# Longer stretches of projection matmuls for the DeltaNet inputs and gates, and the last columns of the final norm's product on GpSimd, in a hybrid attention and DeltaNet block

## The chip, the cores and the metric

The kernel runs on one core of a Trainium2 chip. The metric is the device time of one execution in microseconds. A core has five engines that run at the same time, each with an instruction queue of its own: TensorE (PE in the profile; its weight loads are listed apart as PEld), VectorE (DVE), ScalarE (ACT), GpSimd (POOL) and SyncE (SP), which here issues the transfers between the chip's memory (HBM) and the core's own memories. Those are SBUF, 128 partitions wide, and PSUM, into which TensorE writes.

## The reference

One decoder block for 1,024 tokens of width 1,024. The normed input is projected once. Half of the columns goes through stick-breaking attention with 8 heads, the other half through a gated DeltaNet with 4 heads; both are normed by head, gated, joined and projected back, the input is added, and a last norm follows.

```python
h = rmsnorm(x, norm1_w)
proj = einsum('btd,de->bte', h, w_in)
sb_q, sb_k, sb_v, sb_z, g_q, g_k, g_v, g_z, g_b, g_a = split(proj)

# attention, per query block of 128: A = sigmoid(z) * prod(1 - sigmoid(z) of the keys between)
o_sb = rmsnorm(stick_breaking_attention(sb_q, sb_k, sb_v), sb_norm_w) * silu(sb_z)

# DeltaNet: causal convolution of 4 taps, silu, l2 norm, then chunk by chunk
v_new = u_c - w_c @ state
o_c = (q_c * exp(g_c)) @ state + a_c @ v_new
state = state * exp(g_last) + (k_c * exp(g_last - g_c)).T @ v_new
o_gdn = rmsnorm(o_gdn, gdn_norm_w) * silu(g_z)

x = x + concat(o_sb, o_gdn) @ w_out
return rmsnorm(x, final_norm_w)
```

The kernel takes chunks of 128 tokens in the DeltaNet instead of 64. Everything is in 32-bit floats. The large products run in a reduced form: each operand is split into a high and a low part, and three products replace one.

## The kernel before

**Stages.** The queries (stage Q), half of the values and the decay inputs are projected first. Then a long middle part runs four kinds of work side by side on TensorE: the remaining projections, the DeltaNet's preparation and its recurrence over eight chunks per head, and attention window by window. Last comes the output product, one block of 128 tokens after another, first the DeltaNet's half of the columns, then attention's.

**Projections.** `projections` (line 889) goes through the list `ORDER` (line 29): G0 to G3 are the inputs of the four DeltaNet heads (three blocks of columns each), k0 to k3 the keys, z4 to z7 the gates of the DeltaNet, z0 to z3 the gates of attention, v1 the second half of the values. One block is two halves of 512 tokens; one half is eight steps k of three matmuls each (`mm3`), all into one PSUM buffer `pp` (for G0's second half `pz`). In the order rows they read `pp<-xh,weh`, `pp<-xl,weh` and `pp<-xh,wel`. A half has 24 such matmuls.

**What sets the order.** The program's generators are run by a planner, `interleave` (line 440). It holds a model of the engines with a cost for each operation. Each kind of work is a `Stream` with a priority. A stream runs until its next `yield`; then, when the modelled TensorE has nothing queued, the planner takes the ready stream of best priority. A stream is ready when the results that it waits for have been there in the model for `SLACK` = 450 ns. The projections (`fill`, line 1568) have priority 100, behind the recurrence (0), its preparation and attention (10): they are what TensorE does while the others wait. Where a projection yields is therefore where other work may cut in. Line 942 sets this: after every second step k (six matmuls), for z0 to z3 after every step (three matmuls). The planner's order on TensorE is the order of the program; on the other engines the modelled order is laid down in the same way.

**Names in the middle part.** `gdn_chain` (line 1195) is the recurrence: per chunk `pc<-state,kqf` and `pz<-state,kqf` (products with the state), `pc<-xct,xinv` (the solve), `pz<-v,kn` (the state's update) and `pz<-vr,at` (the output). These are full 32-bit matmuls, which the profile lists as two records each. `window` (line 1291) is attention: `pz<-kh,q` and `pz<-kl,q` are scores, `pz<-step,stf` transposes of the weights (`step` holds the identity), `po<-ah,v2a` and `po<-al,v2a` the products with the values, `pz<-step,otf` the transposes of the output.

**The end.** `products_attention` (line 1517) makes the second half of the output product. For the last block it goes in three pieces of 512, 320 and 192 columns: VectorE adds the piece to the sum in `xr` (`xr<-pp,xr`); ScalarE squares it and sums the squares, for the last piece VectorE (`yj<-xr`, the result in `sy`); and `yf<-xr,fnw` multiplies by the final norm's gain, the first two pieces on GpSimd, the last one on VectorE. GpSimd then takes the root (`ry<-sy,half`), VectorE and ScalarE scale `yf` by it, and two transfers write the block out.

Of the kernel before, what the change touches and what calls it, by code (L numbers as in the profile page):

```python
# [14 lines left out]
ALU = mybir.AluOpType  # L15
# [6 lines left out]
NK = D // P  # L22
# [451 lines left out]
def block(tc, xT_d, x_d, n1_d, wE_d, wQ_d, wC_d, conv_d, alog_d, dtb_d, mixw_d, wo_d, fnw_d, out_d):  # L474
    nc = tc.nc
    ck = Model({"V": nc.vector, "A": nc.scalar, "G": nc.gpsimd, "P": nc.tensor, "S": nc.sync})
    V, A, G, TE, S = ck.V, ck.A, ck.G, ck.P, ck.S

    with ExitStack() as top:
# [36 lines left out]
        def rsqrt(y, a, n):  # L516
            return G.tensor_tensor(y, a, half[:, 0:n], ALU.pow)
# [68 lines left out]
        def mm3(out, lh, ll, rh, rl, start, stop):  # L586
            TE.matmul(out, lh, rh, start=start, stop=False)
            TE.matmul(out, lh, rl, start=False, stop=False)
            TE.matmul(out, ll, rh, start=False, stop=stop)
# [50 lines left out]
        for k in range(NK):  # L640
# [29 lines left out]
            if k:  # L670
                for j in range(8):
                    i, hs = j // 2, slice((j % 2) * 512, (j % 2) * 512 + 512)
# [97 lines left out]
        def values():  # L770
            for b in range(NB):
                yield lambda: ps.room("pp", 2)
                bs = slice(b * P, (b + 1) * P)
                pt = pp()
                for k in range(NK):
                    mm3(pt[:, 0:256], xh[:, k, bs], xl[:, k, bs], chl[k][:, 0, 264:520], chl[k][:, 1, 264:520], k == 0, k == NK - 1)
                    if k % 2 and k < NK - 1:
                        yield
                v_evac(pt, b, 0, 4, 1.0)
                yield  # L780
            flags["v1"] = True
# [107 lines left out]
        def projections():  # L889
            todo = []  # L890
            for step in ORDER:
                if step[0] == "G":
                    h = int(step[1])
                    todo += [(f"G{h}{kind}", lambda: True) for kind in (1, 0, 2)]
                else:
                    todo.append((step, lambda: True))

            def take():
                for n, (name, ok) in enumerate(todo):
                    if ok():  # L900
                        del todo[n]
                        if name[0] == "v":
                            return name, None
                        e = {"k": 0, "z": 16}.get(name[0])
                        e = 4 + 4 * int(name[2]) + int(name[1]) if name[0] == "G" else e + int(name[1])
                        if e == early.e:
                            return name, early
                        cols = Columns(e)
                        cols.load()
                        return name, cols  # L910
                return None

            def split(nxt, n):
                while nxt and nxt[1] and len(nxt[1].hl) < n:
                    nxt[1].split()

            nxt = take()
            split(nxt, 2)
            while nxt:
                name, cols = nxt  # L920
                if name[0] == "v":
                    nxt = take()
                    split(nxt, 2)
                    yield from values()
                    continue
                fill.prio = 100
                for half in range(2):
                    hs = slice(half * 512, (half + 1) * 512)
                    wide = name[:2] == "G0" and half
                    yield lambda: ps.room("pz", 4) if wide else ps.room("pp", 2)  # L930
                    pt = pz() if wide else pp()
                    for k in range(NK):
                        n = 8 * half + k
                        if n == 2:
                            nxt = take()
                        if n == 8:
                            split(nxt, 1)
                        if n == 12:
                            split(nxt, 2)
                        h, l = cols.hl[k // 4]  # L940
                        mm3(pt, h[:, k % 4, :], l[:, k % 4, :], xh[:, k, hs], xl[:, k, hs], k == 0, k == NK - 1)
                        if (k % 2 or name in ('z0', 'z1', 'z2', 'z3')) and k < NK - 1:
                            yield
                    if half == 0:
                        if name[0] == "G":
                            ev = g_evac(int(name[1]), int(name[2]))
                        else:
                            ev = {"k": k_evac, "z": z_evac}[name[0]](int(name[1]))
                    flags[name if half else name + ".0"] = ev(pt, half)
                    yield  # L950
                if nxt is None:
                    nxt = take()
                    if nxt is None and todo:
                        yield lambda: any(ok() for _, ok in todo)
                        nxt = take()
                    split(nxt, 2)
            flags["proj"] = True
# [412 lines left out]
        wts = {}  # L1370
# [56 lines left out]
        def block_tile(b, name):  # L1427
            return pools[0].tile([P, D], F32, tag="xr", bufs=3, name=name) if b < 3 else pools[1].tile([P, D], F32, tag="yr", bufs=5, name=name)
# [88 lines left out]
        def products_attention():  # L1517
            yield lambda: f"d{NB - 1}" in flags
            for b in range(NB):
                last = b == NB - 1  # L1520
                parts = (slice(0, 512), slice(512, 832), slice(832, D)) if last else (slice(0, 512), slice(512, D))
                sy = None
                for got in product(b, 0, parts):
                    if not isinstance(got, tuple):
                        yield got
                        continue
                    n, hs, yp, y = got
                    if sy is None:
                        sy = pools[0].tile([P, 3], F32, tag="sy", bufs=2, name="sy")
                        yf = block_tile(0, "yf") if last else y  # L1530
                    V.tensor_tensor(y[:, hs], yp, y[:, hs], ALU.add)
                    junk = pools[1].tile([P, 584], F32, tag="yj", name="yj")
                    if n == 2:
                        V.scalar_tensor_tensor(junk[:, 0:hs.stop - hs.start], y[:, hs], 1.0 / D, y[:, hs], ALU.mult, ALU.mult, accum_out=sy[:, n:n + 1])
                    else:
                        A.activation(junk[:, 0:hs.stop - hs.start], y[:, hs], AF.Square, scale=D ** -0.5, accum_out=sy[:, n:n + 1])
                    if last and n < 2:
                        G.tensor_tensor(yf[:, hs], y[:, hs], wts["fnw"][:, hs], ALU.mult)
                    if n == 1 and last:
                        G.tensor_tensor(sy[:, 0:1], sy[:, 0:1], sy[:, 1:2], ALU.add)  # L1540
                    elif n:
                        V.scalar_tensor_tensor(sy[:, 0:1], sy[:, 0:1], EPS, sy[:, n:n + 1], ALU.add, ALU.add)
                    if n < len(parts) - 1:
                        yield
                        continue
                    if last:
                        V.tensor_tensor(yf[:, hs], y[:, hs], wts["fnw"][:, hs], ALU.mult)
                    ry = pools[0].tile([P, 1], F32, tag="ry", bufs=2, name="ry")
                    os_ = slice(b * P, (b + 1) * P)
                    if last:  # L1550
                        rsqrt(ry, sy[:, 0:1], 1)
                        V.tensor_scalar(yf[:, 0:640], yf[:, 0:640], ry[:, 0:1], None, ALU.mult)
                        A.activation(yf[:, 640:D], yf[:, 640:D], AF.Copy, scale=ry[:, 0:1])
                        S.dma_start(out_d[os_, 0:640], yf[:, 0:640])
                        nc.scalar.dma_start(out_d[os_, 640:D], yf[:, 640:D])
                    else:
                        rsqrt(ry, sy[:, 0:1], 1)
                        for u in range(2):
                            us = slice(512 * u, 512 * u + 512)
                            yb = (pc, po)[u]()  # L1560
                            A.activation(yb, y[:, us], AF.Copy, scale=ry[:, 0:1])
                            V.tensor_tensor(y[:, us], yb, wts["fnw"][:, us], ALU.mult)
                        S.dma_start(out_d[os_, :], y)
                    ck.free(*ready[b, 0][:2], y)
                    flags[f"a{b}"] = True
                    yield
# [46 lines left out]
```

## Time and profile before

| | |
|---|---|
| median of 3 runs | 648.09 us (647.86 to 648.28) |
| the profiled execution | 648.12 us |
| its span, first to last instruction | 646.0 us |
| granted TensorE clock, mean | 0.999 |
| HBM traffic | 76.03 MB read, 35.03 MB written, 172 GB/s |

The span is what the profile covers; the execution's own time has 2.1 us more around it. In a row of the timeline stand the start in us, the duration in us, the engine, the line, the operation, the tile written and those read, the shape, how many records are merged (x2), and in brackets how long the engine sat idle before and what ended that. Almost all rows carry line 358, where a recorder passes every operation on, so groups are told apart by their tiles. In a row of groups stand the busy time in us and the mean of one in ns, then idle time. In a row of waits stand who waited for whom, us in total, how often, and the longest.

TensorE is busy from the first slice of the span to the last but one. The granted clock is full throughout. The transfers take 53.5% of the 16 DMA engines' time.

### The profile page before, as it was taken

The numbers are of one execution on the slowest core, as the hardware profiler recorded it, in microseconds if no ns is written. First come the engines' busy times: TensorE is split into PE (matmuls) and PEld (weight loads), VectorE is DVE, ScalarE is ACT, GpSimd is POOL, SyncE is SP. The second block draws the span as 40 slices with busy tenths as digits, with TensorE's granted clock in tenths as the row PEclk, the third lists the DMA queues.
The fourth block names the chain that finished last, engine by engine and source line by source line (L and its number), as shares of the span: only waits on it lengthen the run. The fifth ranks groups of instructions, "written<-read, shape, count | busy, mean of one in ns | idle before, by whom it ended". The sixth has DMA issues, their size and how long they took to land.

```text
span 646.0 us, 11666 instructions
## 1 busy us (share of the span) xinstructions
PE 637.4 (99%) x3976; PEld 549.4 (85%) x3976; DVE 425.0 (66%) x779; ACT 394.0 (61%) x945; POOL 339.2 (53%) x428
## 2 busy tenths in 40 slices
PE   8999999999999999999999999999999999999996
PEld 7889988988888898888988888988888887888885
DVE  4469974223897768887658777585774237468864
ACT  5764577724968778787668677585654342132553
POOL 0115056837793668974486955667432232136632
PEclk9999999999999999999999999999999999999999
DMA  8886338766472553654445734636222279773223
GB/s 292 320 282 234 132 118 293 266 206 209 140 228 86 159 182 93 222 157 143 117 150 142 236 116 118 207 101 190 86 62 89 80 247 316 288 227 99 66 102 126
DMA packets 96666, 111.82 MB, mean 173 GB/s; under 512 B 28576, under 2 KB 61536, under 8 KB 96608
## 3 DMA queue, kind: packets, MB, share of 16 engines
q1 hardware_dynamic: 96320, 110.89, 53.5%
q8 instruction: 31, 0.51, 0.3%
q14 instruction: 27, 0.22, 0.1%
q10 hardware_dynamic: 288, 0.20, 0.1%
HBM read 76.03 MB, written 35.03 MB: 172 GB/s over the span
## 4 chain that ended last, share of the span: by engine, by line
PE 92%; DVE 3%; ACT 2%; issue 1%; POOL 1%; DMA 1%; POOLq 0%; SPq 0%; DVEq 0%; ACTq 0%
PE pp L358 54%; PE pz L358 27%; PE po L358 7%; PE pc L358 3%; DVE mgf L358 1%; POOL rsb L358 1%; ACT nkv L358 0%; DMA mgf<-gate_s 0%; DVE ssb L358 0%; DVE xr L358 0%; DVE mf L358 0%; ACT xinv L358 0%; ACT sgf L358 0%; DMA xr<-x 0%; DVE al L358 0%
## 5 line engine op out<-in xcount | busy, mean ns | idle before, releaser
L358 PE MATMUL pp<-xh,weh 128*128 128x512 f32 x360 | 148.1, 411 | 0.0
L358 PE MATMUL pp<-xh,wel 128*128 128x512 f32 x360 | 141.4, 393 | 0.0
L358 PE MATMUL pp<-xl,weh 128*128 128x512 f32 x360 | 140.6, 391 | 0.0
L358 POOL TENSOR_TENSOR sgf<-sgf,cc 128x128 f32<-128x128 f32 (+3 forms) x64 | 77.3, 1210 | 56.9 <-DVE cc L358 52.8
L358 POOL TENSOR_TENSOR wel<-wer,weh 128x512 fp32r<-128x512 f32 x48 | 62.6, 1307 | 74.6 <-ACT weh L358 65.3
L358 PEld LDWEIGHTS pp<-xh,wel 128*128 128x128 f32 x360 | 67.5, 188 | 15.4
L358 PEld LDWEIGHTS pp<-xl,weh 128*128 128x128 f32 x360 | 67.8, 188 | 10.8
L358 PEld LDWEIGHTS pp<-xh,weh 128*128 128x128 f32 x360 | 67.6, 188 | 10.8 <-DVE ac L358 0.2
L358 DVE TENSOR_TENSOR_SCAN cc<-pz,step 128x384 f32<-128x384 f32 (+2 forms) x64 | 53.6, 847 | 13.1 <-ACT pz L358 8.7
L358 DVE TENSOR_TENSOR al<-pz,ah 128x512 fp32r<-128x512 f32 (+1 forms) x80 | 49.6, 631 | 18.9 <-ACT ah L358 18.5
L358 ACT ACTIVATE ah<-pz 128x512 fp32r<-128x512 f32 (+1 forms) x80 | 43.7, 565 | 24.1 <-PE pz L358 23.1
L358 ACT ACTIVATE sgf<-pz,rs 128x384 f32<-128x384 f32 (+3 forms) x96 | 54.5, 601 | 4.9 <-PE pz L358 4.6
L358 ACT ACTIVATE pz<-pz,ns 128x384 f32<-128x384 f32 (+3 forms) x96 | 53.2, 583 | 0.0
L358 PE MATMUL pp<-woh,mh 128*128 128x512 f32 (+2 forms) x132 | 51.8, 393 | 0.6 <-DMA mgf<-gate_s 0.5
L358 PE MATMUL pp<-woh,ml 128*128 128x512 f32 (+2 forms) x132 | 50.9, 386 | 0.0
L358 PE MATMUL pp<-wol,mh 128*128 128x512 f32 (+2 forms) x132 | 50.6, 383 | 0.0
L358 PE MATMUL po<-ah,v2a 128*128 128x256 f32 (+1 forms) x160 | 43.9, 300 | 0.0
L358 POOL TENSOR_TENSOR ml<-mf,mh 128x512 fp32r<-128x512 f32 x16 | 21.5, 1346 | 42.2 <-ACT mh L358 37.7
L358 DVE TENSOR_TENSOR_SCAN cc<-pz,cc,step 128x512 f32<-128x512 f32 (+1 forms) x32 | 38.8, 1213 | 6.8 <-ACT pz L358 5.9
L358 POOL TENSOR_TENSOR ac<-ac,pre 128x512 f32<-128x512 f32 x24 | 31.0, 1290 | 19.1 <-ACT pre L358 12.9
L358 DVE SCALAR_TENSOR_TENSOR pp<-pre,conv,pp 128x512 f32<-128x512 f32 x42 | 31.5, 750 | 13.7 <-ACT pp L358 13.2
L358 PE MATMUL po<-al,v2a 128*128 128x256 f32 (+1 forms) x160 | 38.7, 280 | 0.0
(292 smaller groups left out, 1590.8 us busy)
## 6 DMA issues: line engine op xcount, KB each, us to landing
wer<-wE SPq DMA_DIRECT2D x48, 256.0 KB, 3.5
xr<-x SPq DMA_DIRECT2D x16, 512.0 KB, 7.9
g_s<-ac SPq DMA_DIRECT2D x24, 256.0 KB, 2.4
v_s<-v2e SPq DMA_DIRECT2D x16, 256.0 KB, 2.6
kqf<-g_s SPq DMA_DIRECT2D x16, 256.0 KB, 3.7
v2a<-v_s SPq DMA_DIRECT2D x8, 512.0 KB, 4.8
q<-qk_s SPq DMA_DIRECT2D x8, 512.0 KB, 5.4
kh<-qk_s SPq DMA_DIRECT2D x8, 512.0 KB, 5.0
```

Source lines behind the costliest of these rows:

```text
L358: ins = f(*args, **kw).ins
```

## The change

Two edits. In `projections`, the streams whose name begins with G or z yield after every fourth step k, that is once in a half, after twelve matmuls; the keys k0 to k3 stay at every second step, and z0 to z3 at every step. In `products_attention`, the last block's third piece of `yf<-xr,fnw` (192 columns) goes to GpSimd as the other two do, and VectorE's instruction for it goes away.

```diff
-                        if (k % 2 or name in ('z0', 'z1', 'z2', 'z3')) and k < NK - 1:
+                        if ((k % 4 == 3 if name[0] in 'Gz' else k % 2) or name in ('z0', 'z1', 'z2', 'z3')) and k < NK - 1:
                             yield
...
-                    if last and n < 2:
+                    if last:
                         G.tensor_tensor(yf[:, hs], y[:, hs], wts["fnw"][:, hs], ALU.mult)
...
-                    if last:
-                        V.tensor_tensor(yf[:, hs], y[:, hs], wts["fnw"][:, hs], ALU.mult)
```

The first edit moves instructions on all engines, since the planner's choices follow each other. On TensorE no matmul is added or removed. Three places show it.

In the middle of the recurrence, here for the second head, TensorE's rows before: a recurrence step (the solve, `xct`), six projection matmuls, the next step (`v`, the state's update) and what follows it.

```order
L358 MATMUL pc_4158<-xct_4160,xinv_826 128x128
L358 MATMUL pp_4163<-xh_110,weh_3920 128x512
L358 MATMUL pp_4163<-xl_111,weh_3920 128x512
L358 MATMUL pp_4163<-xh_110,wel_3921 128x512
L358 MATMUL pp_4163<-xh_110,weh_3920 128x512
L358 MATMUL pp_4163<-xl_111,weh_3920 128x512
L358 MATMUL pp_4163<-xh_110,wel_3921 128x512
L358 MATMUL pz_4185<-v2_4172,kn_2102 128x128
L358 MATMUL pz_4189<-state_3986,kqf12_1427 128x128
L358 MATMUL pz_4189<-vr_4093,at_2200 128x128
```

And TensorE's rows of the change in the same head, from the end of one projection stretch of twelve matmuls on.

```order
L358 MATMUL pp_3817<-xh_110,wel_3664 128x512
L358 MATMUL pz_3906<-v2_3853,kn_2125 128x128
L358 MATMUL pz_3910<-vr_3728,at_2232 128x128
L358 MATMUL po_3816<-ah_3785,v2a_3223 128x256
L358 MATMUL po_3816<-al_3786,v2a_3223 128x256
L358 MATMUL po_3816<-ah_3785,v2a_3223 128x256
L358 MATMUL po_3816<-al_3786,v2a_3223 128x256
L358 MATMUL pz_3978<-step_65,stf66_3770 128x128 x3
L358 MATMUL po_3816<-ah_3875,v2a_3223 128x256
L358 MATMUL po_3816<-al_3876,v2a_3223 128x256
```

Between two stretches, more steps of the recurrence and of attention now stand side by side. Over the whole program TensorE has 97 stretches of projection matmuls instead of 125; before, 101 had six matmuls and 12 had twelve, now 15 have six, 49 have twelve, and 22 have three.

At the end of the last head's recurrence, TensorE's rows before: only projections of z0 to z3 lie between the steps.

```order
L358 MATMUL pc_6739<-state_6723,kqf99_4744 128x128
L358 MATMUL pp_6714<-xh_110,weh_6648 128x512
L358 MATMUL pp_6714<-xl_111,weh_6648 128x512
L358 MATMUL pp_6714<-xh_110,wel_6649 128x512
L358 MATMUL pp_6714<-xh_110,weh_6673 128x512
L358 MATMUL pp_6714<-xl_111,weh_6673 128x512
L358 MATMUL pp_6714<-xh_110,wel_6674 128x512
L358 MATMUL pc_6739<-xct_6741,xinv_826 128x128
```

And the same two steps of the last chunk in the change.

```order
L358 MATMUL pc_6686<-state_6674,kqf91_4761 128x128
L358 MATMUL po_6637<-ah_6654,v2a_6444 128x256
L358 MATMUL po_6637<-al_6655,v2a_6444 128x256
L358 MATMUL po_6637<-ah_6654,v2a_6444 128x128
L358 MATMUL po_6637<-al_6655,v2a_6444 128x128
L358 MATMUL pz_6696<-step_65,stf148_6662 128x128 x4
L358 MATMUL pp_6524<-xh_110,weh_6426 128x512
L358 MATMUL pp_6524<-xl_111,weh_6426 128x512
L358 MATMUL pp_6524<-xh_110,wel_6427 128x512
L358 MATMUL pc_6686<-xct_6688,xinv_826 128x128
```

Attention's last windows (`stf`, `ah`, `al`) now share this part with the recurrence; before, they were finished ahead of it.

The third place is GpSimd's end: before, and then in the change.

```order
L358 TENSOR_TENSOR ry_7879<-sy_7858,half_71 128x1
L358 TENSOR_TENSOR yf_7902<-xr_7088,fnw_7295 128x512
L358 TENSOR_TENSOR yf_7902<-xr_7088,fnw_7295 128x320
L358 TENSOR_TENSOR sy_7901<-sy_7901 128x1
L358 TENSOR_TENSOR ry_7943<-sy_7901,half_71 128x1
```

```order
L358 TENSOR_TENSOR ry_7879<-sy_7858,half_71 128x1
L358 TENSOR_TENSOR yf_7902<-xr_7088,fnw_7295 128x512
L358 TENSOR_TENSOR yf_7902<-xr_7088,fnw_7295 128x320
L358 TENSOR_TENSOR sy_7901<-sy_7901 128x1
L358 TENSOR_TENSOR yf_7902<-xr_7088,fnw_7295 128x192
L358 TENSOR_TENSOR ry_7943<-sy_7901,half_71 128x1
```

The product of 192 columns stands ahead of the root in GpSimd's queue. On VectorE it stood between the square-and-sum `yj` and the last sum `sy`, which now follow each other.

## The prediction

> **What bounds the kernel now.** I read the page's first part, then the chain of waits, then what TensorE itself waited for.
>
> ```profile
> span 646.0 us, 11666 instructions
> PE 637.4 (99%) x3976; PEld 549.4 (85%) x3976; DVE 425.0 (66%) x779; ACT 394.0 (61%) x945; POOL 339.2 (53%) x428
> PE 92%; DVE 3%; ACT 2%; issue 1%; POOL 1%; DMA 1%; POOLq 0%; SPq 0%; DVEq 0%; ACTq 0%
> ```
>
> TensorE is busy for 637.4 of 646.0 us and carries 92% of the chain that ended last. Busy matmul time alone is no proof, because records overlap, so the next view is the list of TensorE's waits:
>
> ```profile
> PE po L358 <- DVE step L358: 1.7, 1, 1.7
> PE pp L358 <- DMA mgf<-gate_s: 0.5, 1, 0.5
> PE pz L358 <- DVE al L358: 0.2, 1, 0.2
> ```
>
> Three waits, 2.4 us, and the largest is the start. So the span is the time to the first matmul, then the sum of the distances from one matmul's start to the next, then a tail:
>
> ```profile
> 1.67 3.36 PE L358 MATMUL po<-step 128*128 128x128 f32 x14 [1.67 <-DVE step L358]
> 639.65 0.28 PE L358 MATMUL pp<-woh,ml 128*128 128x192 f32 x1
> ```
>
> From 1.67 to 639.65 are 638.0 us for 3,975 distances; the tail behind it is 646.0 - 639.65 = 6.35 us. The changed kernel has the same 3,976 matmuls in another order. A reordering can gain only if the distances shrink at the seams between kinds of work, and can lose only by a wait that is new. All sums below are against this execution, 648.12 us with 2.1 us around its span; the median of the runs is 648.09, so nothing needs converting.
>
> **The seams, first edit.** The first half of the change lets a projection of the G and z4 to z7 kind run for twelve matmuls instead of six before other work may come in. The order rows say that it does so: projection stretches on TensorE fall from 125 to 97, those of exactly six from 101 to 15, and 49 are now of exactly twelve. What does a stretch cost? This is the last head's recurrence, in which every step comes between two stretches:
>
> ```profile
> 506.60 0.40 PE L358 MATMUL pp<-xh,wel 128*128 128x512 f32 x1
> 506.83 0.38 PE L358 MATMUL pz<-v,kn 128*128 128x128 f32 x2
> 507.05 0.39 PE L358 MATMUL pz<-state,kqf 128*128 128x128 f32 x2
> 507.27 0.39 PE L358 MATMUL pz<-vr,at 128*128 128x128 f32 x2
> 507.42 0.48 PE L358 MATMUL pp<-xh,weh 128*128 128x512 f32 x1
> 507.73 0.39 PE L358 MATMUL pp<-xl,weh 128*128 128x512 f32 x1
> 507.96 0.39 PE L358 MATMUL pp<-xh,wel 128*128 128x512 f32 x1
> 508.20 0.38 PE L358 MATMUL pc<-state,kqf 128*128 128x128 f32 x2
> ```
>
> The first column is the start, and differences of starts are what count. A projection matmul takes 507.96 - 507.73 = 0.23, but the first one behind the recurrence 507.73 - 507.42 = 0.31: a return seems to cost 0.08 to 0.09. But look at the pairs before it. One pair followed by another takes 507.05 - 506.83 = 0.22, and the last pair only 507.42 - 507.27 = 0.15. What the return adds, the pair has saved. A recurrence pair between two projection stretches costs what it costs among its like, and merging such visits saves about nothing. That is the bulk of the stretches that vanish: of returns behind a 128-wide recurrence pair there are 28 before and 11 now.
>
> Transposes do have a price:
>
> ```profile
> 323.05 0.37 PE L358 MATMUL pz<-step,stf 128*128 128x128 f32 x3
> 323.26 0.46 PE L358 MATMUL pp<-xh,weh 128*128 128x512 f32 x1
> 323.56 0.39 PE L358 MATMUL pp<-xl,weh 128*128 128x512 f32 x1
> 323.79 0.39 PE L358 MATMUL pp<-xh,wel 128*128 128x512 f32 x1
> ```
>
> Three transposes take 0.21, 0.07 each, as always, and the first projection behind them 0.30, so leaving a run of transposes costs 0.07. But it costs that whatever follows, and the number of runs of transposes that end in a projection, score, value or recurrence matmul is 112 in both orders (45, 28, 28 and 11 before; 45, 19, 31 and 17 now). So here too the sum is nil.
>
> I summed the seams in two ways. First, each distance was put into a group by the kinds and widths of the matmul before it, itself and the one behind it, and the middle value of each group laid along both orders: 633.9 us before (the real 638.0 has the start's loads and small lateness on top), 632.2 now, so -1.7; 136 of the 3,975 distances had to be borrowed from the nearest group. Second, each seam between two kinds got its measured excess over the kinds' own pace, and the counts were changed: some 14.3 us of seams in all, and -0.4 for the new counts. The difference between the two is the borrowed groups. I take the middle, **-1.1 us**, with -1.7 and +0.3 as ends (the borrowed distances scatter by 0.05 each, 0.6 over 136).
>
> [...]
>
> **The tail, second edit.** The last 192 columns of the norm's product leave VectorE and go to GpSimd, behind the last block's sum. What stands there now:
>
> ```profile
> 637.66 1.30 POOL L358 TENSOR_TENSOR yf<-xr,fnw 128x512 f32<-128x512 f32 x1 [1.10 <-DVE xr L358]
> 638.69 0.48 DVE L358 TENSOR_TENSOR xr<-pp,xr 128x320 f32<-128x320 f32 x1
> 639.25 0.87 POOL L358 TENSOR_TENSOR yf<-xr,fnw 128x320 f32<-128x320 f32 x1 [0.29 <-DVE xr L358]
> 639.97 0.36 DVE L358 TENSOR_TENSOR xr<-pp,xr 128x192 f32<-128x192 f32 x1 [0.80 <-PE pp L358]
> 640.08 0.20 POOL L358 TENSOR_TENSOR sy<-sy 128x1 f32<-128x1 f32 x1
> 640.46 0.36 DVE L358 SCALAR_TENSOR_TENSOR yj<-xr 128x192 f32<-128x192 f32 x1
> 640.74 0.08 DVE L358 DVE_READ_ACCUMULATOR yj<-xr 128x1 f32 x1
> 640.74 0.35 DVE L358 TENSOR_TENSOR yf<-xr,fnw 128x192 f32<-128x192 f32 x1
> 641.01 0.15 DVE L358 SCALAR_TENSOR_TENSOR sy<-sy 128x1 f32<-128x1 f32 x1
> 641.25 0.54 POOL L358 TENSOR_TENSOR ry<-sy,half 128x1 f32<-128x1 f32 x1 [0.97 <-DVE sy L358]
> 641.82 0.61 ACT L358 ACTIVATE yf<-yf,ry 128x384 f32<-128x384 f32 x1 [1.99 <-POOL ry L358]
> ```
>
> Everything from the root (ry at 641.25) on is the same in both kernels; the question is when ry can start. On VectorE the product delays the sum sy from about 640.95 (0.13 behind the accumulator's 640.82, the distance from xr's end at 640.33 to yj) to 641.01: 0.06. Without a clash, that is all that moving it gains. On GpSimd 512 columns take 1.30 and 320 take 0.87, so 192 take 0.87 - 128 x 0.43/192 = 0.58. GpSimd starts 0.08 behind VectorE's add (639.17 to 639.25), so at 640.41, and ends at 640.99. VectorE's square-and-sum yj, both inputs in SBUF, is due at 640.46, in the middle of it. That the two exclude each other the output stage shows:
>
> ```profile
> 601.88 0.16 DVE L358 SCALAR_TENSOR_TENSOR sy<-sy 128x1 f32<-128x1 f32 x1 [0.85 <-ACT yj L358]
> 613.89 1.29 POOL L358 TENSOR_TENSOR ml<-mf,mh 128x512 fp32r<-128x512 f32 x1 [1.39 <-ACT mh L358]
> 614.11 1.09 DVE L358 SCALAR_TENSOR_TENSOR sy<-sy 128x1 f32<-128x1 f32 x1
> ```
>
> The same one-column sum takes 0.16 alone and 1.09 beside a GpSimd product, ending 0.02 behind it (615.20 against 615.18), that is 0.14 less than its own time later. So yj would end at 640.99 + 0.36 - 0.14 = 641.21, the sum start 0.13 later and end at 641.49, and ry start 0.09 behind that, at 641.58 instead of 641.25: **+0.33**. If VectorE comes first, GpSimd holds ry back to about 641.35: +0.10. If they did not exclude each other: -0.06. I take +0.33, since GpSimd's release is the shorter by 0.05; ends -0.06 and +0.33.
>
> [...]
>
> **The sum:** 648.12 - 1.1 + 0.33 = **647.3 us**. That is 0.8 us or 0.12% under the time before, inside the 0.2% (1.3 us) that a measurement of this kernel can tell from no change.
>
> **The rivals.** *The returns cost what they seem to.* The triple's first matmul has the longer records:
>
> ```profile
> L358 PE MATMUL pp<-xh,weh 128*128 128x512 f32 x360 | 148.1, 411 | 0.0
> L358 PE MATMUL pp<-xl,weh 128*128 128x512 f32 x360 | 140.6, 391 | 0.0
> ```
>
> 20 ns x 360 = 7.2 us over 125 returns are 0.06 each, and measured by starts a whole stretch takes 0.10 longer than its matmuls at their pace. For 28 returns fewer that gives -1.6 to -2.8, with the tail 646.9 to 645.7. Against it stands the short last pair. For it: the grouped sum came out at -1.7.
>
> *A new wait on TensorE; this is the side of slower.* Its place is the end of the last head's recurrence. By the order rows and the distances, attention's last score products move from about 468 to 496 us, while the recurrence ends at 509 instead of 513; before, it had those last 40 us nearly for itself:
>
> ```profile
> 160.00:180.00 20.00, 20.00 (x106) 16.61 (x105) 16.05 (x25) 17.82 (x38) 15.65 (x19) 1.00 0.40 114
> 480.00:500.00 20.00, 20.00 (x134) 18.02 (x133) 9.38 (x21) 8.75 (x27) 2.95 (x5) 1.00 0.21 66
> ```
>
> (Columns: stretch, length, then busy time of PE, PEld, DVE, ACT, POOL.) ScalarE at 8.75 of 20 us would go to the 17 or 18 of the densest stretch, and the only cover there is z0 to z3, which give way every three matmuls, 0.7 us. If six of the last steps each wait 0.5 us, as the output stage's one wait did, that is 3 us: 650.3. It decides from about 2.1 us of new waits. Against it: at 17.82 of 20 us ScalarE made TensorE wait nowhere before, and the shortest distances between a recurrence step and the one that needs its VectorE result are alike in both orders (1.2 us).
>
> That the change would not do what it says is ruled out by the order rows.
>
> **How the numbers follow.** Forecast, within 0.2%: 0.44. Returns that cost what they seem to, with a gain of over 1.3 us: 0.35. New waits that make it slower by over 1.3 us: 0.21. The forecast's own range, from the ends -1.7 - 0.06 and +0.3 + 0.33 with half a microsecond of small waits on top, is 646.3 to 649.3. The range asked for reaches to 645.4 (most of the first rival) and to 650.0 (into the second), and leaves out the rest, some 2 in 10.
>
> **What would show it.** Seams: the sum of distances from first to last matmul falls by about 1 us, with the last start near 638.6; a projection behind a recurrence pair still takes 0.31. Tail: yj on VectorE takes 0.7 instead of 0.36 or starts late, and ry starts 1.9 us behind the last matmul's start instead of 1.60. Wrong: TensorE's list of waits holds more than 4 us, above all at 470 to 515 us, or the distances fall by 2 us or more.

## The result and the profile after

| | before | after |
|---|---|---|
| median | 647.89 us (647.19 to 648.36, 13 runs) | 646.54 us (645.89 to 646.97, 13 runs) |
| ratio, 95% interval | 1 | 0.9978 (0.9970 to 0.9987) |
| span of the profiled execution | 646.0 us | 644.7 us |
| first matmul to last, by starts | 638.0 us | 636.4 us |
| last matmul's start to the end of the span | 6.35 us | 6.67 us |

The last row is worked out from spans given to 0.1 us, here and below.
The changed kernel is 1.35 us faster, 0.2%; 647.3 us were forecast. The head of the page of the changed kernel, and TensorE's list of waits (who waited for whom, us in total, times, longest):

```profile
span 644.7 us, 11693 instructions
PE 635.5 (99%) x3976; PEld 551.4 (86%) x3976; DVE 430.3 (67%) x778; ACT 392.8 (61%) x943; POOL 340.5 (53%) x429
```

```profile
PE po L358 <- DVE step L358: 1.7, 1, 1.7
PE pp L358 <- DVE v2e L358: 0.6, 1, 0.6
PE pz L358 <- DVE oe L358: 0.2, 1, 0.2
```

TensorE still sets the time, and its list of waits is as short as before: 2.5 us against 2.4. The rival of new waits did not come to pass. The 0.6 us for `v2e` lies in the second half of the values, at 118.5 us; in a second trace with the same order of matmuls (the new yields alone, below) it is missing, so it is scatter.

The price of a return to a projection is what the prediction read from before. From the changed kernel's timeline of TensorE (start, duration):

```profile
304.58 0.40 PE L358 MATMUL pp<-xh,wel 128*128 128x512 f32 x1
304.81 0.39 PE L358 MATMUL pz<-v,kn 128*128 128x128 f32 x2
304.96 0.47 PE L358 MATMUL pp<-xh,weh 128*128 128x512 f32 x1
305.27 0.40 PE L358 MATMUL pp<-xl,weh 128*128 128x512 f32 x1
```

The pair takes 0.15 instead of its 0.22, the projection behind it 0.31 instead of 0.23: 0.46 together, 0.01 more than each among its like.

The tail in the changed kernel, from the last matmul on:

```profile
638.03 0.28 PE L358 MATMUL pp<-woh,ml 128*128 128x192 f32 x1
638.34 0.36 DVE L358 TENSOR_TENSOR xr<-pp,xr 128x192 f32<-128x192 f32 x1 [0.80 <-PE pp L358]
638.78 0.59 POOL L358 TENSOR_TENSOR yf<-xr,fnw 128x192 f32<-128x192 f32 x1
638.84 0.75 DVE L358 SCALAR_TENSOR_TENSOR yj<-xr 128x192 f32<-128x192 f32 x1
639.69 0.16 DVE L358 SCALAR_TENSOR_TENSOR sy<-sy 128x1 f32<-128x1 f32 x1
639.93 0.54 POOL L358 TENSOR_TENSOR ry<-sy,half 128x1 f32<-128x1 f32 x1 [0.56 <-DVE sy L358]
```

GpSimd's product takes 0.59 (0.58 was estimated). VectorE's square `yj` is stretched from 0.36 to 0.75 and ends 0.22 behind GpSimd, so the root `ry` starts 1.90 us behind the last matmul's start instead of 1.60. So the second edit costs 0.3 us, and the first has brought 1.6 us of distances. What are these 1.6 us?

### The profile page after: what moved, and what is told of

It is laid out like the page before. It is cut to its first block, busy times and chain, and to the rows that moved or that the text cites. A ratio compares the mean times of both kernels' runs of the same rounds, so it can differ in the third digit from the quotient of the medians.

```text
span 644.7 us, 11693 instructions
## 1 busy us (share of the span) xinstructions
PE 635.5 (99%) x3976; PEld 551.4 (86%) x3976; DVE 430.3 (67%) x778; ACT 392.8 (61%) x943; POOL 340.5 (53%) x429
## 4 chain that ended last, share of the span: by engine, by line
PE 90%; DVE 3%; POOL 3%; issue 1%; ACT 1%; DMA 1%; SPq 0%; POOLq 0%; DVEq 0%; ACTq 0%
PE pp L358 52%; PE pz L358 27%; PE po L358 8%; PE pc L358 3%; DMA dt<-cum_s 1%; DVE cc L358 1%; POOL wel L358 1%; POOL rsb L358 1%; SPq L358 0%; POOL tm L358 0%; DVE ssb L358 0%; POOL ac L358 0%; POOL xs L358 0%; DVE mgf L358 0%; ACT sgf L358 0%
## 5 line engine op out<-in xcount | busy, mean ns | idle before, releaser
L358 PE MATMUL pp<-xh,weh 128*128 128x512 f32 x360 | 146.0, 405 | 0.0
```

The lines of the kernel that those rows point to most:

```text
L358: ins = f(*args, **kw).ins
```

## The experiments

### Each edit alone, and the opposite of the first

The new yields with the old tail, and the old yields with the new tail:

```diff
-                        if (k % 2 or name in ('z0', 'z1', 'z2', 'z3')) and k < NK - 1:
+                        if ((k % 4 == 3 if name[0] in 'Gz' else k % 2) or name in ('z0', 'z1', 'z2', 'z3')) and k < NK - 1:
```

> The new yields alone, with the last product of 192 columns left on VectorE. Theory A (the tail costs what the row of after shows, 6.67 us from the last matmul's start to the end of the span instead of 6.35, and the matmuls' distances are those of the change): 0.3 us less than the whole change, so about 646.2 us, a ratio to before near 0.9974; distances 636.4 us from the first to the last matmul's start, tail 6.35 us. Theory B (the tail's 0.32 us is scatter of one execution): the time of the whole change, 646.5 us.

```diff
-                    if last and n < 2:
+                    if last:
...
-                    if last:
-                        V.tensor_tensor(yf[:, hs], y[:, hs], wts["fnw"][:, hs], ALU.mult)
```

> The old yields, only the last product of 192 columns moved to GpSimd. Theory A: TensorE's order is that of before, so the distances stay near 638.0 us (within 0.4 us), and the tail grows from 6.35 to 6.67 us: 0.3 us slower than before, about 648.2 us, ratio 1.0005. Theory B (product on GpSimd beside the square is worth something): not slower than before. [...]

Measured: 646.43 us, ratio 0.9982 (0.9973 to 0.9991), for the yields alone; distances 636.7, tail 6.39. And 648.23 us, ratio 1.0009 (1.0000 to 1.0018), for the tail alone; distances 637.5, tail 6.66. Theory A holds for the tail in both traces. The times are too coarse to tell it from theory B: the yields alone have the ratio 0.9982, the whole change 0.9978. The distances of one order scatter by up to half a microsecond between traces, nearly all of it in the projections of queries and values: the queries, whose order no yield touches, took 44.9 us in before, 44.2 in the change, 45.6 with the yields alone. Without the matmuls of queries and values, two traces of one order agree within 0.1 us (545.87 and 545.84 with the old yields, 544.50 and 544.40 with the new). There the gain is 1.4 us, and that is the number to explain.

```diff
-                        if (k % 2 or name in ('z0', 'z1', 'z2', 'z3')) and k < NK - 1:
+                        if (name[0] in 'Gz' or k % 2) and k < NK - 1:
```

> The opposite of the change: DeltaNet inputs and gates give way after every three matmuls, keys after six as before, z0 to z3 after six instead of three is not meant: they give way after every second step here as the keys do. The tail is that of before. 157 stretches of projection matmuls instead of 125 (97 in the change). Theory A (a return to a projection is about free; what counts is which kinds of matmul stand beside each other): the middle values of before and after, kind by kind with their neighbours, summed over this order give 0.2 to 0.4 us more than before, so 648.1 to 648.3 us, with a few tenths of single late starts either way. Rival 1 (each return costs 0.06 to 0.10 us): 32 returns more, 1.9 to 3.2 us slower than before, 649.8 to 651.1 us.

(z0 to z3 give way after three matmuls here as in before; the sentence on them above is mistaken, the 157 stretches are right.) Measured: 648.96 us, ratio 1.0017 (1.0007 to 1.0026), distances 639.0. Slower by 0.5 to 1.7 us: less than rival 1 asks, more than theory A does. On average a stretch more or less is worth 0.03 to 0.05 us in these runs. Whether that is a price of the return is tested below.

### The wait ahead of the output product

In before the list of waits has one of 0.5 us for `mgf<-gate_s`, a load, just ahead of the first output matmul (546.59); in the change it is gone. The start of that matmul is 0.85 behind the one before it in before and 0.24 in the change: 0.6 of the 1.4 us. What that matmul needs is a free buffer `pp`, and so that VectorE has read it (`zt`, the gates' product). TensorE's rows of before, then VectorE's:

```profile
545.74 0.39 PE L358 MATMUL pp<-xh,wel 128*128 128x512 f32 x1
546.59 0.47 PE L358 MATMUL pp<-woh,mh 128*128 128x512 f32 x1 [0.47 <-DMA mgf<-gate_s]
```

```profile
545.09 0.69 DVE L358 TENSOR_TENSOR mf<-pz,mgf 128x512 f32<-128x512 f32 x1 [2.06 <-POOL ml L358]
545.70 0.68 DVE L358 TENSOR_TENSOR zt<-pp,zs 128x512 f32<-128x512 f32 x1
```

`zt` ends at 546.38, 0.21 ahead of the matmul. It stands behind `mf`, the split of the third output block, which sat 2.06 us until GpSimd's `ml` of the second block was through. If that is the cause, holding back the third block's split alone must take the wait away:

```diff
-                yield lambda: ("in", b, g) in ready and (b < 3 or f"{'ad'[g]}{b - 3}" in flags) and (b > 2 or g or f"d{5 + b}" in flags)
+                yield lambda: ("in", b, g) in ready and (b != 2 or "d0" in flags) and (b < 3 or f"{'ad'[g]}{b - 3}" in flags) and (b > 2 or g or f"d{5 + b}" in flags)
```

> Before, with one thing changed: the DeltaNet half of the third output block is split only when the first block's product is through, so that VectorE's gate product (zt) no longer stands behind that block's product (mf), which itself stands behind GpSimd. Nothing of TensorE's order ahead of 538 us changes, and the yields and the tail are those of before. Theory W (0.6 us of the change's gain is the wait ahead of the output product, 0.62 us in before, 0.01 in after, and it is VectorE's zt that lets the buffer go): that distance falls from 0.85 to 0.23-0.25 us, the distances from 638.0 to about 637.4, the time by 0.6 to about 647.2 us. Theory S (the gain is the seams): nothing to be had here, 647.7 to 647.9 us. Theory D (it is the load of the gates that was waited for, as the list of waits names it): the wait stays at 0.5 us.

TensorE and VectorE at that place in this kernel:

```profile
544.75 0.40 PE L358 MATMUL pp<-xh,wel 128*128 128x512 f32 x1
544.99 0.39 PE L358 MATMUL pp<-woh,mh 128*128 128x512 f32 x1
```

```profile
541.72 0.69 DVE L358 TENSOR_TENSOR mf<-pz,mgf 128x512 f32<-128x512 f32 x1 [0.60 <-issue]
542.79 0.69 DVE L358 TENSOR_TENSOR zt<-pp,zs 128x512 f32<-128x512 f32 x1 [0.38 <-DMA gate_s<-zt]
```

`zt` comes 2.9 us earlier and the matmul follows after 0.24 us: theory W. The load that the list named was not the cause. One other candidate moved with `zt`: ScalarE's `mh` of the third block, which in before ended at 546.45, 0.14 us ahead of the matmul. Against it speaks, as an argument and not as a test, that the first output matmul reads the first block's `mh`, which was through at 537.81, and that with 460 ns (below) the same wait stands ahead of a projection, which reads no `mh`, 0.05 us behind `zt`. The time is 647.00 us, ratio 0.9992 (0.9983 to 1.0000). By the trace 0.5 us is kept: the output product has one start 0.63 us late here (610.30, waiting for `xr`), where before has one 0.26 late (605.36).

### Other orders: is it the number of stretches?

Orders of very different stretches, with the tail of before. One number of the planner:

```diff
-SLACK = 450
+SLACK = 460
```

> A reshuffle without any aim: the planner holds a stream back for 460 ns instead of 450 ns after its operands; yields and tail are those of before. 123 stretches of projection matmuls instead of 125. Theory A (the change's gain is a small change of the seams' kinds and which starts happen to be late): the seams' middle values sum to 0.2 to 0.3 us less than before, single late starts come and go by up to 1 us, so 647 to 648.6 us. Rival 1 (returns are what is paid): two returns fewer, 0.1 to 0.2 us faster, 647.7 us.

Keys give way every twelve matmuls too; then the gates z0 to z3 every six:

```diff
-                        if (k % 2 or name in ('z0', 'z1', 'z2', 'z3')) and k < NK - 1:
+                        if (k % 4 == 3 or name in ('z0', 'z1', 'z2', 'z3')) and k < NK - 1:
```

> The yields of the change, and the keys' projections give way every twelve matmuls too; the tail is that of before. 91 stretches of projection matmuls instead of 97. Theory A (what counts are the kinds side by side and single late starts): 123 runs of transposes to leave instead of 129, and by the groups' middle values 0.1 to 0.4 us less than the yields alone, so 646.0 to 646.3 us if no start is late, and up to 1 us more where some are. Rival 1 (0.05 us each, what 28 stretches fewer and 32 more have shown on average): 6 stretches fewer, 0.3 us, 646.1 us. Rival 2 (an order without its tuned slack makes TensorE wait, as 460 ns instead of 450 ns did with 5.7 us): several us slower.

```diff
-                        if (k % 2 or name in ('z0', 'z1', 'z2', 'z3')) and k < NK - 1:
+                        if (k % 4 == 3 if name[0] in 'G' or name in ('z4','z5','z6','z7') else k % 2) and k < NK - 1:
```

> The yields of the change, and the gates z0 to z3 give way every six matmuls instead of three; the tail is that of before. 89 stretches of projection matmuls instead of 97, none of three. Theory A: the groups' middle values give 0.1 to 0.25 us less than the yields alone, 646.2 to 646.4 us. Rival 1 (0.05 us a stretch): 0.4 us less, 646.0 us. Rival 2 (the last head's recurrence and attention's last windows now wait behind longer stretches, and ScalarE is dense there): new waits on TensorE at 470 to 515 us, over 1 us slower.

Measured: 654.67 us (ratio 1.0108, 1.0094 to 1.0121), 649.82 (1.0029, 1.0020 to 1.0038) and 654.48 (1.0102, 1.0089 to 1.0116). All three missed theory A and rival 1. New waits came, as rival 2 had it for the last two; but with the gates every six not at the 470 to 515 us that it named. From the lists of TensorE's waits, first with 460 ns, then with the gates every six:

```profile
PE pp L358 <- DVE zt L358: 3.1, 1, 3.1
PE pp L358 <- POOL wel L358: 2.1, 2, 1.2
```

```profile
PE pz L358 <- DVE mgf L358: 3.9, 1, 3.9
PE pz L358 <- DMA mgf<-gate_s: 0.7, 1, 0.7
```

The longest of them lie between 542 and 550 us, where the last projections pass into the output product. VectorE with 460 ns:

```profile
544.42 0.69 DVE L358 TENSOR_TENSOR mf<-pz,mgf 128x512 f32<-128x512 f32 x1 [2.03 <-POOL ml L358]
545.03 0.68 DVE L358 TENSOR_TENSOR zt<-pp,zs 128x512 f32<-128x512 f32 x1
```

That is the wait of before, grown to 3.1 us: `zt` behind `mf` behind `ml`. The change has the same chain, and only its time makes it free:

```profile
542.27 0.69 DVE L358 TENSOR_TENSOR mf<-pz,mgf 128x512 f32<-128x512 f32 x1 [2.07 <-POOL ml L358]
542.88 0.68 DVE L358 TENSOR_TENSOR zt<-pp,zs 128x512 f32<-128x512 f32 x1
```

There `zt` is through 1.45 us ahead of the first output matmul at 545.01.

Three more, run once each: eighteen matmuls for G and z4 to z7, no yield inside the halves of z4 to z7, and 470 ns.

```diff
-                        if (k % 2 or name in ('z0', 'z1', 'z2', 'z3')) and k < NK - 1:
+                        if ((k == 5 if name[0] in 'Gz' else k % 2) or name in ('z0', 'z1', 'z2', 'z3')) and k < NK - 1:
```

> DeltaNet inputs and gates z4 to z7 give way once in a half, after eighteen matmuls; keys, z0 to z3 and the tail as before. 96 stretches. What is read is the middle part of the trace (everything between the values and the output product) without its starts that are 0.2 us or more late: before 449.9 us with 125 stretches, the change's yields 448.5 with 97, three matmuls 451.3 with 157. Theory stretches (0.045 us each): 448.5. Theory stalls (the weight loads that could not run ahead, 24 small late starts of 2.2 us in before, 10 of 1.1 in the change, 33 of 3.3 with three matmuls; the kinds side by side are worth 447.1 in before and change alike): the middle follows the sum of the small late starts whatever the number of stretches, kinds 447.1 to 447.8. The whole time is uncertain by several us, since the passage to the output product differs with every order.

```diff
-                        if (k % 2 or name in ('z0', 'z1', 'z2', 'z3')) and k < NK - 1:
+                        if ((k % 4 == 3 if name[0] == 'G' else name[0] == 'k' and k % 2) or name in ('z0', 'z1', 'z2', 'z3')) and k < NK - 1:
```

> The yields of the change, but the gates z4 to z7 do not give way inside a half at all (24 matmuls); tail as before. 103 stretches. Theory stretches: middle part 448.9 us. Theory stalls: 447.1 to 447.8 plus the small late starts, as many as the weight loads' waits tell. Time between 646 and 653 us, by the passage to the output product.

```diff
-SLACK = 450
+SLACK = 470
```

> Before with the planner's slack at 470 ns instead of 450 ns, yields and tail as before. 129 stretches. Theory stretches: middle part 450.1 us. Theory stalls: more slack means that operands are there earlier, so fewer small late starts than the 24 of before, middle part under 449.9. Time between 647 and 655 us, by the passage to the output product (460 ns took 654.7).

Measured: 658.76, 653.44 and 645.10 us, one run each, beside 648.25 for before; the last two lie outside the times expected (646 to 653 and 647 to 655).

The table takes the distances apart. A group is a matmul's kind and width with those of its two neighbours, and its middle value is taken over all fourteen traces. The sums run over the same 2,939 matmuls in every order, those that are neither queries, values nor output product. (The expectations' 449.9 for before is a narrower count of the same trace.) The columns are:

- Kinds: the sum of the groups' middle values.
- Small late starts: those 0.05 to 0.2 us over their group's middle value.
- Later ones: starts that are later still, in this middle part and around the output product.
- At half clock: what the matmuls lost in stretches in which the granted clock was one half (see the end; with the gates every six a wait of 0.7 us is in it).
- Middle: all time of the middle part without the last three columns.

| order | stretches | middle, us | kinds, us | small late starts | later ones, middle | around output | at half clock |
|---|---|---|---|---|---|---|---|
| before | 125 | 450.8 | 448.0 | 24, 2.2 us | 0.5 | 0.9 | 0 |
| the change | 97 | 449.5 | 448.0 | 10, 1.1 us | 1.1 | 0.3 | 0 |
| three matmuls | 157 | 452.2 | 448.7 | 34, 3.4 us | 0.9 | 0.0 | 0 |
| 460 ns | 123 | 450.2 | 447.6 | 19, 1.9 us | 6.2 | 0.6 | 1.6 |
| keys twelve | 91 | 449.7 | 447.8 | 17, 1.7 us | 0.5 | 3.1 | 1.6 |
| gates six | 89 | 448.8 | 447.7 | 8, 0.9 us | 1.1 | 5.4 | 3.4 |
| eighteen | 96 | 451.5 | 448.4 | 31, 3.1 us | 10.2 | 0.0 | 1.5 |
| gates never | 103 | 449.9 | 447.8 | 18, 1.9 us | 1.2 | 4.1 | 1.5 |
| 470 ns | 129 | 449.9 | 448.1 | 14, 1.3 us | 0.3 | 0.0 | 0 |

The kinds differ by 1.1 us over orders with 89 to 157 stretches, and by nothing between before and the change. The middle part goes with the small late starts in all nine.

Does it go with the number of stretches? At 0.045 us each from the 450.8 of before, the theory of stretches asks for 449.5, 449.8 and 451.0 in the last three. The gates that never give way (449.9) are where it puts them; eighteen is 2.0 us over, 470 ns 1.1 under. The other orders lie within half a microsecond of it. So fewer stretches mostly come with fewer small late starts, but a stretch has no fixed price: in the two orders where stretches and late starts part, the time goes with the late starts. 129 stretches make the fastest of these orders, 96 the slowest.

That the columns, with what lies under 0.05 us, add up is how they are made; the finding is which of them moves. With coarser groups, in which the three matmuls of a triple count as one kind and the scores, the value products and the transposes as one each, the kinds are 446.8 in before and 446.7 in the change, the small late starts 3.8 and 2.8 us. The row of keys twelve is from an execution of 651.4 us, the longest of its eleven.

### What a small late start is

It does not stand in the list of TensorE's waits, but it does in that of its weight loads. From that list of before, then of the change:

```profile
PEld pz L358 <- issue: 4.3, 13, 0.4
PEld pz L358 <- DVE al L358: 2.0, 6, 0.6
PEld pz L358 <- DVE cc L358: 1.3, 5, 0.3
```

```profile
PEld pz L358 <- issue: 1.8, 5, 0.4
PEld pz L358 <- DVE cc L358: 1.2, 5, 0.4
```

"issue" is time for which the profile shows nothing that was waited for. All rows for `pz` together are 28 waits of 9.0 us in before and 18 of 5.4 in the change. Of these, 14 and 9 (5.3 and 3.2 us, most of the "issue" rows among them) stand ahead of the preparation's smaller matmuls (weights of 32x32 or 128x64), where only one of the 24 small late starts of before lies; the others, 3.7 and 2.2 us, are the ones to look at. Most of such a gap costs nothing, as matmuls run on meanwhile: beside the 9.0 us of before the small late starts sum to 2.2. How one looks from near is seen in the kernel with three matmuls, where the same step comes with a late start and without. First the matmuls, then the weight loads of the same two places:

```profile
216.64 0.39 PE L358 MATMUL pp<-xh,wel 128*128 128x512 f32 x1
216.99 0.49 PE L358 MATMUL pz<-v,kn 128*128 128x128 f32 x2
217.24 0.48 PE L358 MATMUL pp<-xh,weh 128*128 128x512 f32 x1
...
223.43 0.39 PE L358 MATMUL pp<-xh,wel 128*128 128x512 f32 x1
223.66 0.38 PE L358 MATMUL pz<-v,kn 128*128 128x128 f32 x2
223.79 0.48 PE L358 MATMUL pp<-xh,weh 128*128 128x512 f32 x1
```

```profile
216.99 0.30 PEld L358 LDWEIGHTS pz<-v,kn 128*128 128x128 f32 x2 [0.39 <-DVE cc L358]
```

```profile
223.50 0.35 PEld L358 LDWEIGHTS pz<-v,kn 128*128 128x128 f32 x2
```

For the pair at 223.66 the weight load began 0.16 us ahead of it; at 216.99 the load was held back until the pair itself could start. The pair then starts 0.12 late and takes 0.25 instead of 0.13: 0.2 us for a result that came just too late. It is the rule: of the 175 small late starts of the nine orders 169 (23 of 24 in before, all 10 in the change) have a weight load that began no more than 0.03 us ahead of its matmul, either their own or that of the matmul just before; of all distances of the middle part one in five has. In before most of the small late starts, 14 of 24, are scores followed by scores; in the change 4 of 10.

At 223.50 the load ran beside the projection matmul that had started at 223.43 and is listed for 0.39 us; at 216.99 the load came 0.35 us behind the start of the matmul ahead of it, and the 0.2 us are what was lost there.

### The tail without the clash

```diff
-                    if n == 2:
-                        V.scalar_tensor_tensor(junk[:, 0:hs.stop - hs.start], y[:, hs], 1.0 / D, y[:, hs], ALU.mult, ALU.mult, accum_out=sy[:, n:n + 1])
-                    else:
+                    if True:
                         A.activation(junk[:, 0:hs.stop - hs.start], y[:, hs], AF.Square, scale=D ** -0.5, accum_out=sy[:, n:n + 1])
```

> The whole change, with the last piece's square and sum (yj, 192 columns) on ScalarE instead of VectorE. Theory A (VectorE's square waits for GpSimd's product, ScalarE's would not): 320 columns take 0.47 and 512 take 0.62, so 192 take 0.37; with a start 0.09 behind the add (638.79) and 0.10 for the accumulator it is through at 639.26, but the sum sy on VectorE still waits for GpSimd's end at 639.37 and ends 0.02 behind it; ry then starts 1.45 us behind the last matmul's start instead of 1.90, and the time is 0.45 us under the change's, about 646.1. Rival (ScalarE stands still beside GpSimd as well): yj takes 0.7 us, ry at 1.9 us, 646.5 us.

```profile
637.39 0.28 PE L358 MATMUL pp<-woh,ml 128*128 128x192 f32 x1
638.14 0.59 POOL L358 TENSOR_TENSOR yf<-xr,fnw 128x192 f32<-128x192 f32 x1
638.15 0.36 ACT L358 ACTIVATE yj<-xr 128x192 f32<-128x192 f32 x1 [0.58 <-DVE xr L358]
638.71 0.16 DVE L358 SCALAR_TENSOR_TENSOR sy<-sy 128x1 f32<-128x1 f32 x1 [0.65 <-ACT yj L358]
638.95 0.54 POOL L358 TENSOR_TENSOR ry<-sy,half 128x1 f32<-128x1 f32 x1 [0.22 <-DVE sy L358]
```

On ScalarE the square takes 0.36 beside GpSimd's 0.59, and `ry` starts 1.56 us behind the last matmul: theory A, 0.1 short of its gain, since `sy` started 0.10 behind the end of ScalarE's accumulator (638.61). The tail is 6.31 us, the time 645.71, ratio 0.9968 (0.9956 to 0.9981). Beside the same product the square took 0.75 on VectorE; the runs show these two times, and not what holds VectorE up.

Last, this tail with the order of 470 ns and the old yields:

```diff
-SLACK = 450
+SLACK = 470
```

> Before with the planner's slack at 470 ns and the tail with GpSimd's product and the square on ScalarE; the yields are those of before (129 stretches). If the gain of the 470 ns order (distances 635.1 us in its one profile, against 638.0) is a property of the order and not of that execution, and the tail gives 0.04 to 0.1 us on top: 645.0 us, a ratio to before of 0.996. If it was scatter: within 0.6 us of before.

Measured: 645.64 us, ratio 0.9969 (0.9958 to 0.9981), distances 635.2. The gain belongs to the order, not to one execution. This kernel and the one above beat before. From the change (0.9978, 0.9970 to 0.9987) and from each other the intervals don't separate them; their traces are shorter, with spans of 643.2 and 643.7 us against 644.7.

## Why the prediction came out as it did

**The time.** 647.3 us against 646.5; the sign of both terms was right and their size near (-1.1 and +0.33 forecast, -1.6 and +0.32 in the trace, of which -0.25 lies in the queries and values, where traces of one order differ by more). The measured gain of 1.35 us lies on the line of 1.3 that the prediction drew between its forecast and its first rival, so the time alone can't choose between these two.

**The tail** was right in each step: GpSimd's 0.59, `yj` held up beside it at 0.75, `ry` at 1.90. Both traces with the edit, and the one that takes the square away from VectorE, show it.

**The price of a return** was right: 0.31 behind a pair that is 0.07 shorter. Rival 1 took the longer record for a cost. Its price of 0.06 to 0.10 us a return asked for 1.9 to 3.2 us with 32 stretches more, where 0.5 to 1.7 was measured, and eighteen and 470 ns show that there is no fixed price at all.

**The seams' term** failed, though its number came out near. The step was "-1.1, the middle of -1.7 and -0.4". The kinds of neighbours are worth 0.0 between the two orders. The -1.7 had been laid over the groups of one trace, of which 160 out of 346 have one or two members, so that late starts of before could sit in their middle values; that this makes up the -1.7 is likely, not shown. In its place the runs show: small late starts 2.2 to 1.1 us (-1.1), the wait behind `zt` ahead of the output product gone (-0.6), later starts in the middle part 0.5 to 1.1 (+0.6), and under 0.05 us each some -0.2: together -1.3 of the 1.4. The wait behind `zt` is tested by its own run; the small late starts are an account of the traces, and no run took them away alone.

**"Can gain only if the distances shrink at the seams, and can lose only by a wait that is new"** failed with it. That sentence rested on the list of matmul waits, 2.4 us; waits that could go were there: the 0.5 us ahead of the output product in that very list, which the sum put at nothing, and 3.7 us ahead of full-sized matmuls in the list of weight loads, part of them on the path.

**Rival 2** had a real mechanism at the wrong place. In the change nothing waits at 470 to 515 us; around 545 us four of the orders lost 3 to 5 us in waits and 1.5 to 3.4 more at half clock. The change was lucky there: its neighbours, keys twelve and gates six, were not.

**What stays open:** why this order has 10 small late starts and its neighbours 8, 17 or 31. That longer stretches leave the other engines more time was only argued: most orders fit it, the ones with eighteen and with 470 ns speak against it as a rule.

## What to carry to other kernels

Where one engine is busy 99% of the time and has no waits in its own list, look at the list of its weight loads before adding up prices of seams: a load that could not run ahead cost about 0.1 us here, and 8 to 34 of them, 0.9 to 3.4 us, set most of what these orders differed by in the middle part apart from the long waits. Before judging an order, run a neighbour or two: 10 ns of the planner's slack moved this kernel by 7 us and another 10 by almost 10 back, so that a change of 1.4 us says little on whether the idea behind it is good. Look for the one place where many orders pay (here the passage to the output product), and mend that.

## What the runs showed of the hardware

A pause of TensorE can be dearer than its length: behind the 3.07 us wait of the kernel with 460 ns another 1.4 us went. The rows:

```profile
545.76 0.50 PE L358 MATMUL pp<-xh,weh 128*128 128x512 f32 x1 [3.07 <-DVE zt L358]
546.10 0.39 PE L358 MATMUL pp<-xl,weh 128*128 128x512 f32 x1
...
547.39 0.63 PE L358 MATMUL pp<-xh,weh 128*128 128x512 f32 x1
547.82 0.63 PE L358 MATMUL pp<-xl,weh 128*128 128x512 f32 x1
...
549.95 0.63 PE L358 MATMUL pp<-xh,weh 128*128 128x512 f32 x1
550.38 0.45 PE L358 MATMUL pp<-xl,weh 128*128 128x512 f32 x1
550.66 0.40 PE L358 MATMUL pp<-xh,wel 128*128 128x512 f32 x1
```

The matmuls resume at their pace of 0.23, and 1.3 us later go to 0.43 for the seven distances from 547.39 to 550.38: 1.4 us more on top of the wait. The windows of the same trace (stretch, length, busy time of PE, PEld, DVE, ACT, POOL, granted clock, share of the DMA engines, GB/s) show why:

```profile
545.00:547.00 2.00, 1.24 (x5) 1.05 (x6) 1.25 (x3) 1.23 (x2) 1.15 (x1) 1.00 0.54 127
547.00:550.00 3.00, 3.00 (x9) 2.33 (x8) 2.49 (x13) 0.00 (x0) 0.15 (x1) 0.51 0.83 292
```

The granted clock falls to one half (0.51 from 547 to 550). By the traces' records of the clock it does so in five of the nine orders while matmuls run, for 3.41 us each, with the gates every six for 6.83. The waits of TensorE just ahead of it were 3.07 us here, 3.88 and 0.69 with the gates every six, 2.54 where z4 to z7 never give way, but only 1.11 and 0.68 with keys twelve (clock 0.51 from 547.9 to 551.4) and 0.66 and 1.17 with eighteen (0.51 from 186.8 to 190.3). Single waits of up to 1.25 us (460 ns, at 362 us) left the clock full. So ahead of it stood a wait of 2.54 to 3.88 us in three of these orders, and two of 0.66 to 1.17 close together in the other two. What sets it off, and what ends it after 3.41 us, the runs do not show.
